# Attention with keys on partitions: a guard pass for the row maximum, row sums from TensorE, and no DMA transposes

## The chip, the core and the metric

One core of one Trainium2 chip. The metric is the device time of one execution in microseconds; the kernel before takes 1498.41 us, the median of three runs (1491.61 to 1501.3). Engines are named as the profile names them: PE (TensorE matmul; PEld its weight loads), DVE (VectorE), ACT (ScalarE), POOL (GpSimd), SP (SyncE, which here only issues DMAs).

## What is computed

One encoder layer for one sequence of 1024 tokens, width 1024, all in float32. After a conditioned RMSNorm, one projection feeds two groups of eight heads: latent attention (query and key of 96, value of 64, chunk-causal over all keys) and band attention (head size 64, nine chunks of 64 keys, with a relative-position bias). Both use

```
s = einsum('bqhd,bkhd->bhqk', q, k) * scale    (+ bias in the band)
s = where(mask, s, -1e30)
o = einsum('bhqk,bkhd->bqhd', softmax(s), v)
```

An output projection and a gated MLP with a short convolution (inner width 2816) follow. The change touches the attention alone.

## The kernel before, in words

Every float32 product is made as three passes of f32r matmuls over a high and a low half (hi x hi, hi x lo, lo x hi); gemm3 (line 147) does this for the projections.

The attention stage is written as 32 units of 512 queries: 16 of the band (4 head pairs, two halves of the queries, two heads) and 16 of latent attention (8 heads, two halves). A unit has four tiles of 128 queries. For a tile, scores (line 637) makes the scores with queries on partitions: three matmul passes per run of up to 512 keys into a two-bank PSUM tile (tag S, two of them, line 659); DVE adds the bias and finds the row minimum of the negated scores (lines 670, 674, 678), ACT takes the exponential with that minimum as its bias and the row sum as its accumulator (line 684). DVE then makes 2^15/sum (lines 686, 687), POOL makes the high f16 half (line 701), DVE the low one (line 704), and one DMA transpose on SP's queue turns both so that keys lie on partitions (line 706). Three tiles later (DEPTH), values (line 710) multiplies them with V: V's high and low f16 halves are the stationary operand side by side, and the two turned halves of P pass by, 128 queries a matmul (line 717). The four tiles share one PSUM bank (tag pv); ACT and DVE add its two halves up and scale them (lines 724, 725), and the result goes to DRAM.

q and k pages are turned by PE (qk_page, line 615; tag T, one bank) and split into halves by ACT and DVE; a band page holds both heads of a pair.

Between the tiles stand fillers, generators that issue a few matmuls of other work at a time: the projections of q, k and v for later heads (f_qk, f_v), of the latents (f_m), the up-projections (f_up, two groups), and the half of the output projection that needs the band heads only (f_oca). pace (line 806) lets R_CA or R_MLA times an attention tile's estimated cost of filler follow it; need forces a filler that the next unit depends on. The order on each engine is then set when the program is built: a scheduler takes these instructions, with the priorities given by high_priority, and lays down one fixed queue for each engine. On the chip each queue runs in order.

The attention stage ends when the last latent head is done; then come the rest of the output projection (to about 787 us) and the MLP.

## Time and profile before

| | |
|---|---|
| median of three runs | 1498.41 us (1491.61 to 1501.3) |
| span of the profiled execution, which is its own time | 1494.5 us |
| PE busy | 1286.2 us, 86% |
| DVE busy | 1022.1 us, 68% |
| POOL busy | 846.2 us, 57% |
| ACT busy | 610.9 us, 41% |
| DMA queue q1 | 185.18 MB, 44.3% of 16 engines' span |
| DMA transposes | 152, issued by SP |

The profile's page has busy time for each engine, the span in 40 slices, the chain that ended last, and groups of equal instructions with their busy time, mean duration, and the idle time ahead of them with what ended it. In a group's row the tile names stand without their buffer numbers: sc and sm are scores of the band and of latent heads, Pc and Pm the exponentials, hlc and hlm the f16 halves, PTc and PTm the turned ones, pvc and pvm the value products, oc and om the results (oc is also the name of the half output projection's PSUM tile), ipq, ipv, mp, qu, ku the fillers' products. A line such as L71, L75 or L82 is that of a helper that scales, or makes a high or a low half.

### The profile page before, as it was taken

What the parts mean: (1) busy time and instruction counts of PE and PEld (TensorE: products, weight loads), DVE (VectorE), ACT (ScalarE), POOL (GpSimd) and SP (SyncE); (2) the same over time, 40 slices, a digit from 0 to 9 for tenths busy, and PEclk for the clock granted to TensorE, in tenths of its full rate; (3) what the DMA queues carried; (4) which work ended last, traced back from release to release, by engine and by line L of the source; (5) the groups of instructions that cost most, each with busy time, mean ns of one, the idle gap of its engine ahead of it and who ended that gap; (6) DMA issues with size and microseconds to landing.
All of it is one profiled execution on the core that took longest, in us unless ns stands there. A gap on an engine that the chain in (4) does not pass through costs nothing.

```text
span 1494.5 us, 20136 instructions
## 1 busy us (share of the span) xinstructions
PE 1286.2 (86%) x6804; PEld 1067.4 (71%) x6804; DVE 1022.1 (68%) x1663; ACT 610.9 (41%) x1183; POOL 846.2 (57%) x868
## 2 busy tenths in 40 slices
PE   3789999998667888876929769999999999999997
PEld 2679878887546666664717548888888887887885
DVE  8844777756658777753576657877777787566653
ACT  5543444343445554532444224444444443333331
POOL 5664454563699744433866145655555555665662
PEclk9979989997678798977958979999999999999999
DMA  8334567554412677778521142222222234446442
GB/s 315 116 80 94 116 133 160 134 115 98 96 36 52 145 151 168 157 139 263 178 86 57 69 145 83 85 85 85 85 85 82 78 130 167 150 142 244 149 141 98
DMA packets 218738, 186.45 MB, mean 125 GB/s; under 512 B 148102, under 2 KB 183050, under 8 KB 218636
## 3 DMA queue, kind: packets, MB, share of 16 engines
q1 hardware_dynamic: 218636, 185.18, 44.3%
q8 instruction: 53, 0.87, 0.2%
q14 instruction: 49, 0.40, 0.1%
HBM read 121.69 MB, written 28.84 MB: 101 GB/s over the span
## 4 chain that ended last, share of the span: by engine, by line
PE 27%; POOL 13%; DMA 12%; DVE 12%; issue 8%; ACT 2%; SPq 1%; DVEq 0%; POOLq 0%; ACTq 0%
POOL wds L82 4%; PE p L967 3%; PE p L965 3%; PE p L966 3%; DMA wu<-w_up 3%; DMA PTm<-hlm 3%; PE dnp L1037 2%; PE dnp L1038 2%; PE dnp L1039 2%; DVE u L973 2%; PE sm L659 2%; DVE wu L995 1%; DVE u L974 1%; POOL wf L82 1%; DMA cl<-oT_d 1%
## 5 line engine op out<-in xcount | busy, mean ns | idle before, releaser
L82 POOL TENSOR_TENSOR wds<-wd,wds 128x512 fp32r<-128x512 f32 x88 | 153.3, 1760 | 99.3 <-ACT wds L75 99.3
L1037 PE MATMUL dnp<-wds,g 128*128 128x512 f32 x308 | 119.8, 391 | 3.6 <-DVE c L999 1.5
L1027 DVE TENSOR_TENSOR wd<-wd,gmbc 128x1024 f32<-128x1024 f32 x44 | 68.7, 1562 | 76.9 <-DMA wd<-w_down 76.9
L1038 PE MATMUL dnp<-wds,g 128*128 128x512 f32 x308 | 119.7, 389 | 0.0
L1039 PE MATMUL dnp<-wds,g 128*128 128x512 f32 x308 | 118.3, 389 | 0.6 <-DVE g L82 0.6
L75 ACT ACTIVATE wds<-wd 128x512 fp32r<-128x512 f32 x88 | 54.6, 624 | 150.1 <-PE dnp L1039 147.2
L82 POOL TENSOR_TENSOR wc<-ws,wc 128x512 fp32r<-128x512 f32 x22 | 56.0, 2545 | 74.2 <-ACT wc L75 74.2
L71 POOL TENSOR_SCALAR hlc<-Pc,ric 128x640 f16<-128x640 f32 (+2 forms) x64 | 48.1, 754 | 83.6 <-DVE ric L687 22.1
L71 POOL TENSOR_SCALAR hlm<-Pm,rim 128x512 f16<-128x512 f32 (+4 forms) x88 | 59.2, 676 | 62.9 <-DMA PTm<-hlm 45.8
L82 POOL TENSOR_TENSOR wa<-wu,wa 128x512 fp32r<-128x512 f32 x22 | 32.5, 1475 | 91.6 <-ACT wa L75 91.6
L659 PE MATMUL sm<-mk,mq 96*128 96x512 f32 (+3 forms) x288 | 75.8, 399 | 8.8 <-ACT Pm L684 8.4
L704 DVE SCALAR_TENSOR_TENSOR hlm<-Pm,rim,hlm 128x512 f16<-128x512 f32 (+4 forms) x88 | 66.7, 765 | 24.1 <-POOL hlm L71 23.7
L717 PE MATMUL pvm<-PTm,vt 128*128 128x128 f16 x576 | 53.2, 248 | 33.6 <-DMA PTm<-hlm 28.5
L431 DVE SCALAR_TENSOR_TENSOR aacc<-aw,cs,aacc 128x256 f32<-128x256 f32 x84 | 49.2, 586 | 47.6 <-DMA aw<-w_ada 47.1
L973 DVE SCALAR_TENSOR_TENSOR u<-c,pk,u 128x1023 f32<-128x1023 f32 x44 | 75.5, 1723 | 4.4 <-ACT u L972 4.4
L82 DVE TENSOR_TENSOR g<-gr,g 128x512 fp32r<-128x512 f32 x44 | 71.4, 1626 | 9.5 <-ACT g L75 9.5
L717 PEld LDWEIGHTS <-vt 128*128 128x128 f16 x576 | 43.0, 113 | 47.2 <-issue 45.1
L684 ACT ACTIVATE Pc<-sc,mc 128x640 f32<-128x640 f32 (+2 forms) x64 | 42.1, 659 | 76.2 <-DVE mc L674 59.1
L659 PE MATMUL sc<-k,q 64*128 64x512 f32 (+3 forms) x288 | 67.8, 364 | 2.6 <-ACT Pc L684 1.7
L1037 PEld LDWEIGHTS dnp<-wds,g 128*128 128x128 f32 x308 | 57.8, 188 | 17.2 <-ACT wds L75 1.9
L659 PEld LDWEIGHTS sm<-mk,mq 96*128 96x128 f32 x288 | 54.8, 220 | 19.4 <-ACT Pm L684 13.0
L1039 PEld LDWEIGHTS dnp<-wds,g 128*128 128x128 f32 x308 | 57.8, 188 | 13.0 <-DVE g L82 1.0
(352 smaller groups left out, 4340.9 us busy)
## 6 DMA issues: line engine op xcount, KB each, us to landing
wu<-w_up SPq DMA_DIRECT2D x44, 512.0 KB, 3.5
wd<-w_down SPq DMA_DIRECT2D x44, 512.0 KB, 3.4
aw<-w_ada SPq DMA_DIRECT2D x96, 128.0 KB, 2.3
g_d<-u SPq DMA_DIRECT2D x22, 512.0 KB, 2.6
gr<-g_d SPq DMA_DIRECT2D x44, 256.0 KB, 3.5
x<-x SPq DMA_DIRECT2D x16, 512.0 KB, 6.1
adaw<-w_ada_a SPq DMA_DIRECT2D x16, 512.0 KB, 5.0
wq_r<-w_qk SPq DMA_DIRECT2D x32, 128.0 KB, 2.6
```

Of the source, the lines that this page charges most:

```text
L71: pool.tensor_scalar(o, i, s, 1.0, op0=MUL, op1=MUL)
L75: act.activation(o, i, AF.Copy)
L82: (pool if eng == "p" else dve).tensor_tensor(o, i, f32(hi), op=SUB)
L431: dve.scalar_tensor_tensor(acc[:], w[:], cs[:, k:k + 1], acc[:], op0=MUL, op1=ADD)
L659: last = pe.matmul(s[:, c:c + w], qpg[rs_, a, q], kpgs[kh][rs_, b, ko:ko + w], start=(a == 0 and b == 0), stop=(a == 1))
L704: dve.scalar_tensor_tensor(hl[:, w:2 * w], pp, ri[:], hl[:, :w], op0=MUL, op1=SUB)
L717: last = pe.matmul(u.pv[:, c], u.vst(j), mov, start=(x == 0), stop=(x == len(todo) - 1))
L973: dve.scalar_tensor_tensor(u[:, 1:], c[:, :S - 1], pk[:, cv + 1:cv + 2], u[:, 1:], op0=MUL, op1=ADD)
L1027: dve.tensor_tensor(raw[:], raw[:], gmbc[:], op=MUL)
L1037: pe.matmul(pts[t][n], sh, w[n][:, 0], start=(j == 0), stop=False)
L1038: pe.matmul(pts[t][n], sh, w[n][:, 1], start=False, stop=False)
L1039: pe.matmul(pts[t][n], sl, w[n][:, 0], start=False, stop=(j == NF - 1))
```

## The change

Scores are made with keys on partitions, so that P needs no turning. For that the row maximum has to be known ahead:

- guard: for each tile of 128 queries one pass hi x hi over its keys, with queries on partitions as before, into one two-bank tile (tag S, now one buffer). In the band a bias in f32r is added by an identity matmul. DVE writes the tile's minimum into a column of mz.
- mrow: four PE transposes turn these columns into one row, and ACT writes it, with the logarithm of PSCALE, into a further row of the query page; the key page holds ones there, so that a score matmul subtracts the maximum.
- st: for each block of 128 keys one PSUM bank (tag ST, two buffers) of up to 512 queries. A band head stacks k's high and low half on 128 partitions against q's high half twice, so that two passes do; bias (two halves) and mask are matmuls too. A latent head takes three passes, and a mask matmul on the diagonal. ACT takes the exponential of the bank into f32; every second block it takes it a second time into f16 as high half, for the others POOL copies it. DVE makes the low half. P is not normalised.
- val: V's page holds [v, ones] in high and [v, zeros] in low, so that the value product, with up to 512 queries as moving operand and three passes, also makes the row sums. At a unit's end ACT takes Ln and then Exp of minus that for 1/sum, and DVE scales the result.
- prep: band pages are now made for each head by itself; the guard, the row and the pages of the next unit are issued among the blocks of the present one. A unit's queries use one of two page buffers, keys one of three.
- DEPTH, R_CA and R_MLA have other values; the rotary tables move to another pool; the start's PSUM tiles are shared out anew; the second band bias table is an input of its own; f_oca waits for the last band value product; an instruction asks for an activation table that holds both Exp and Ln.

The core of the diff (removed lines are shown where they are short; scores and values above are the removed functions):

```diff
-DEPTH = 3
-OFF_S, OFF_P, OFF_V = 400, 200, 200
-P_BUFS, HL_BUFS, PT_BUFS, TB = 3, 3, 3, 1
-MODE_C = "1111"
-MODE_M = "1111"
-PSCALE, VSCALE = 2.0 ** 15, 2.0 ** 14
-R_CA, R_MLA = 1.9, 0.5
+DEPTH = 2
+OFF_S, OFF_V = 400, 200
+TB = 1
+HI_ON, HL_BUFS = "pa", 3
+PSCALE, VSCALE = 2.0 ** 4, 2.0 ** 14
+R_CA, R_MLA = 1.17, 0.42
...
     startp.__exit__(None, None, None)
+    act.preload_act_table_set("natural_log_exp_and_others")
...
+    def v_tile(pl, name, tag, bufs):
+        v = pl.tile([P, 4, 2, 3, 64], F16, name=name, tag=tag, bufs=bufs)
+        pool.memset(v[:, :, 0, 1], 1.0)
+        pool.memset(v[:, :, 1, 1], 0.0)
+        return v
+
+    def v_set(v, x, src, sc):
+        hi, lo = v[:, x, 0, 0:3:2], v[:, x, 1, 0:3:2]
+        act.activation(hi, src, AF.Copy, scale=sc)
+        for c in range(2):
+            dve.scalar_tensor_tensor(lo[:, c], src[:, c], sc, hi[:, c], op0=MUL, op1=SUB)
...
+    def turned(src, rows, nm):
+        pt = ps.tile([P, 512], F32, name=f"{nm}_ps", tag="T", bufs=TB)
         for j in range(4):
             pe.transpose(pt[:rows, j * P:(j + 1) * P], src(j), ident[:])
-        pg = at.tile([P, 2, 512], F32R, name=name, tag=tag, bufs=bufs)
-        if gain is None:
-            act.activation(pg[:rows, 0], pt[:rows], AF.Copy)
-            dve.tensor_tensor(pg[:rows, 1], pt[:rows], f32(pg[:rows, 0]), op=SUB)
-        else:
-            act.activation(pg[:rows, 0], pt[:rows], AF.Copy, scale=gain)
-            dve.scalar_tensor_tensor(pg[:rows, 1], pt[:rows], gain, f32(pg[:rows, 0]), op0=MUL, op1=SUB)
-        return pg
+        return pt
...
+            order = [0, 1, 2, 3] if g == 0 else ([3, 4, 2, 5, 1, 6, 0, 7] if band else list(range(8)))
+            u.blocks = [(b, max(b, 4 * g), min(b + 4, 4 * g + 3) if band else 4 * g + 3) for b in order]
...
+        def guard(u, j):
...
+                s = ps.tile([P, 1024], F32, name=f"s{u.nm}_{i}", tag="S", bufs=1)
+                last = None
+                for x, (c, ko, w, kh) in enumerate(segs):
+                    last = pe.matmul(s[:, c:c + w], u.q[:rows, 0, q], kpages[u.nm, kh][:rows, 0, ko:ko + w],
+                                     start=True, stop=True)
+                if u.band:
+                    bg = biases[u.hd][0]
+                    w = min(n, 256)
+                    pc = [(c0 + n - w, 256 - w, w)] if (n1 == 0 or n1 >= 256) else \
+                        [(c0 + n - 256, 0, 128), (c0 + n - 128, 128, 128)]
+                    for c, bo, w in pc:
+                        last = pe.matmul(s[:, c:c + w], identr[:], bg[:, bo:bo + w], start=False, stop=True,
+                                         skip_group_check=True)
+                trail.append(last.ins)
+                if u.band:
+                    if i >= 4:
+                        dve.memset(s[64:128, c0:c0 + 64], BIG)
+                else:
+                    dve.memset(s[0:64, c0 + n - 64:c0 + n], BIG)
+                dve.tensor_reduce(mz[:, QK + j:QK + j + 1], s[:, c0:c0 + n], axis=AX.X, op=MIN)
+            return sum(w / 2.4 + 12 for _, _, w, _ in segs) + (110 if u.band else 0)
+
+        def mrow(u):
+            r = u.row
+            with tc.high_priority(offset=OFF_S):
+                pt = turned(lambda j: mz[:, QK + j - r:QK + j + 1], r + 1, f"mr{u.nm}_{u.g}")
+                act.activation(u.q[r:r + 1, u.slot], pt[r:r + 1], AF.Identity, scale=-1.0, bias=nlps[r:r + 1])
+            return 4 * 110
+
+        def st(u, x):
...
+                s = ps.tile([P, 512], F32, name=f"t{nm}", tag="ST", bufs=2)
+                todo = []
+                if u.band:
+                    todo.append((0, w, kt[:, 0, kc], u.q[:, 0, qc]))
+                    todo.append((0, w, kt[:r + 1, 1, kc], u.q[:r + 1, 1, qc]))
+                    if b >= t0:
+                        bt = biases[u.hd][1]
+                        wb = min(256, w)
+                        todo += [(0, wb, identr[:], bt[:, a, :wb]) for a in range(2)]
+                    elif b + 1 >= t0:
+                        bt = biases[u.hd][1]
+                        todo += [(0, P, identr[:], bt[:, a, P:2 * P]) for a in range(2)]
+                    if t1 == b + 4:
+                        todo.append((w - P, w, mk_k[:], mk_q[:]))
+                else:
+                    todo.append((0, w, kt[:r + 1, 0, kc], u.q[:r + 1, 0, qc]))
+                    todo.append((0, w, kt[:r, 0, kc], u.q[:r, 1, qc]))
+                    todo.append((0, w, kt[:r, 1, kc], u.q[:r, 0, qc]))
+                    if b >= t0:
+                        todo.append((0, P, mk_k[:], mk_q[:]))
+                todo.append(todo.pop(1))
+                for y, (c0, c1, l, m) in enumerate(todo):
+                    last = pe.matmul(s[:, c0:c1], l, m, start=(y == 0), stop=(y == len(todo) - 1))
+                trail.append(last.ins)
+                p = at.tile([P, 512], F32, name=f"p{nm}", tag="P", bufs=2)
+                act.activation(p[:, :w], s[:, :w], AF.Exp, scale=-1.0)
+                hl = at.tile([P, 2, 512], F16, name=f"hl{nm}", tag="HL", bufs=HL_BUFS)
+                cnt[0] += 1
+                if HI_ON[cnt[0] % len(HI_ON)] == "a":
+                    act.activation(hl[:, 0, :w], s[:, :w], AF.Exp, scale=-1.0)
+                else:
+                    hi_of("p", hl[:, 0, :w], p[:, :w])
+                dve.tensor_tensor(hl[:, 1, :w], p[:, :w], hl[:, 0, :w], op=SUB)
+                u.hl[x] = hl
+            return sum(max(107, (c1 - c0) / 2.4 + 12) for c0, c1, _, _ in todo)
+
+        def val(u, x):
...
+            w1, w2 = (v[:, y, a, u.odd:u.odd + 2].rearrange("p c b -> p (c b)") for a in range(2))
+            hl = u.hl.pop(x)
+            with tc.high_priority(offset=OFF_V):
+                if x == 0:
+                    u.pv = ps.tile([P, 512], F32, name=f"pv{u.nm}_{u.g}", tag="pv", bufs=1)
+                end = x == len(u.blocks) - 1
+                pe.matmul(u.pv[:, c], w1, hl[:, 0, :w], start=(x == 0), stop=False)
+                pe.matmul(u.pv[:, c], w1, hl[:, 1, :w], start=False, stop=False)
+                last = pe.matmul(u.pv[:, c], w2, hl[:, 0, :w], start=False, stop=end)
+                trail.append(last.ins)
+                if end:
+                    ri = at.tile([P, 512], F32, name=f"ri{u.nm}_{u.g}", tag="ri", bufs=1)
+                    r0, r1 = (slice(64, 128), slice(0, 64)) if u.odd else (slice(0, 64), slice(64, 128))
+                    act.activation(ri[r0], u.pv[r1], AF.Ln)
+                    act.activation(ri[r0], ri[r0], AF.Exp, scale=-1.0)
+                    dve.scalar_tensor_tensor(ri[r0], u.pv[r0], vscale[u.vs][1][r0], ri[r0], op0=MUL, op1=MUL)
+                    sp.dma_start(u.dst_d[:, u.g * 512:(u.g + 1) * 512], ri[r0])
+            return 3 * (w / 2.4 + 3)
...
+                pt = turned(head(0), 64, f"q{p}{o}_{g}")
+                act.activation(u.q[0:64, 0], pt[0:64], AF.Copy)
+                act.activation(u.q[64:128, 0], pt[0:64], AF.Copy)
+                dve.tensor_tensor(u.q[0:64, 1], pt[0:64], f32(u.q[0:64, 0]), op=SUB)
+                pt = turned(head(128), 64, f"k{p}{o}_{g}")
+                gk = gk_ca[0:64]
+                act.activation(u.k[0:64, 0], pt[0:64], AF.Copy, scale=gk)
+                hi_of("p", u.k[0:64, 1], f32(u.k[0:64, 0]))
+                dve.scalar_tensor_tensor(u.k[64:128, 0], pt[0:64], gk, f32(u.k[0:64, 0]), op0=MUL, op1=SUB)
+            return 8 * 110
...
+    for n, u in enumerate(units):
+        tasks = []
+        if n + 1 < U:
+            v = units[n + 1]
+            tasks += [lambda v=v: ready(v)] + [lambda j=j, v=v: v.guard(j) for j in range(4)] + [v.mrow]
+        nb = len(u.blocks)
+        ratio = R_CA if u.band else R_MLA
+        for x in range(nb):
+            cost = u.st(x)
+            late.append((u, x))
+            if len(late) > DEPTH:
+                cost += value()
+            if not late[0][0].band:
+                ca_done.append(1)
+            while len(tasks) > 6 * (nb - 1 - x) // nb:
+                cost += tasks.pop(0)()
+            pace(cost, ratio)
```

275 lines of the change are left out of this document (131 added, 144 removed).

## The prediction

> **What bounds the kernel now.** I read the page's slices first, then the busy time of each engine by stage, then the costliest groups and the waits inside the attention stages, because the change touches those alone.
>
> ```profile
> span 1494.5 us, 20136 instructions
> ...
> PE   3789999998667888876929769999999999999997
> ...
> PEclk9979989997678798977958979999999999999999
> DMA  8334567554412677778521142222222234446442
> ```
>
> ```profile
> core 0: us, PE busy (x) PEld busy (x) DVE busy (x) ACT busy (x) POOL busy (x), PEclk, DMA share, GB/s
> 70.00:120.00 50.00, 39.96 (x272) 34.55 (x271) 20.99 (x67) 24.26 (x68) 28.32 (x38) 0.83 0.36 79
> 120.00:300.00 180.00, 172.25 (x1332) 153.31 (x1331) 127.87 (x369) 75.20 (x186) 88.89 (x106) 0.96 0.58 128
> 300.00:387.00 87.00, 74.80 (x415) 63.82 (x415) 54.78 (x149) 35.01 (x115) 47.50 (x99) 0.81 0.53 115
> 387.00:490.00 103.00, 72.57 (x349) 57.22 (x350) 68.66 (x177) 51.23 (x125) 87.84 (x166) 0.78 0.22 48
> 490.00:686.00 196.00, 156.43 (x1016) 125.83 (x1014) 133.22 (x324) 90.07 (x187) 93.17 (x117) 0.84 0.75 158
> ...
> 1240.00:1494.00 254.00, 240.89 (x1056) 197.85 (x1056) 150.40 (x106) 77.36 (x128) 144.71 (x84) 0.99 0.45 156
> ```
>
> Each slice is 37.4 us. Attention runs from 70 to 686 us: band attention with the projections as filler work up to 387, the up-projections (up0, up1) at 387 to 490, latent attention with the half output projection (oc) as filler behind. The reader should see that no engine bounds all of these 616 us. PE is nearly full at 120 to 300; POOL is the fullest at 387 to 490 (87.8 of 103); at 490 to 686 none is, while the DMA engines are at 0.75 and the clock at 0.84. What waits there:
>
> ```profile
> POOL hlm L71 <- DMA PTm<-hlm: 45.8, 34, 3.8
> PE pvm L717 <- DMA PTm<-hlm: 28.5, 23, 4.0
> ...
> PE pvc L717 <- DMA PTc<-hlc: 15.0, 13, 2.7
> ```
>
> So the DMA transposes hold PE for 28.5 + 15.0 us directly. The question is whether losing them is worth more than what TensorE and ScalarE get instead.
>
> **TensorE's price per matmul.** Busy time of pipelined matmuls overlaps, so I count issue time, start to start, at full clock.
>
> ```profile
> 131.25 0.28 PE L151 MATMUL ipq<-wq_s,hT 128*128 128x256 f32 x1
> 131.37 0.28 PE L152 MATMUL ipq<-wq_s,hT 128*128 128x256 f32 x1
> ...
> 246.19 0.84 PE L717 MATMUL pvc<-PTc,v 128*128 128x128 f16 x12
> ...
> 600.49 0.60 PE L619 MATMUL mq_ps<-ident,qn 128*96 128x128 f32 x4
> ```
>
> 256 columns f32: 0.12 us. 512 columns: 240.89/1056 = 0.228 (last stage above). 384: between, 0.174. 128 columns f16: (0.84-0.22)/11 = 0.056; wider f16 moving operands have no row, and I take 0.056 for each 128 columns (0.224 at 512, beside f32's 0.228). 128 columns f32, transposes too: (0.60-0.27)/3 = 0.11.
>
> **TensorE, part by part**, with counts from the two programs' instruction lists (both 30 key blocks by query tiles a band head, 36 a latent head, 528 in all):
> - Scores before: band 72 each of 128, 256, 384 and 512 columns, 72 x 0.632 = 45.5; latent 48 each of the first three and 144 of 512, 52.2. Values: 1056 x 0.056 = 59.1. Transposes of q and k: 192 x 0.11 = 21.1. Sum 178 us.
> - Guard pass after: band 48, 72, 24, 24 (bias matmuls included), 23.6; latent 16, 16, 16, 48, 17.4. Scores with keys on partitions: band two passes in place of three, but two bias and a mask matmul on many blocks, 128, 144, 48, 48, 50.7; latent 112, 48, 48, 144, 59.2. Values: three passes in place of two, 3 x 528 x 0.056 = 88.7. Transposes: 256 for q and k (a band head now has its own pages) and 128 for the row maximum, 384 x 0.11 = 42.2. Sum 282 us.
>
> That is 104 us more for PE, all inside attention. The other work there stays:
>
> ```profile
> L151 PE MATMUL ipq<-wq_s,hT 128*128 128x256 f32 x192 | 56.9, 296 | 0.0
> ...
> L151 PE MATMUL oc<-wo,ch 128*128 128x512 f32 x64 | 28.7, 451 | 4.7 <-ACT ch L75 4.6
> ...
> L151 PE MATMUL mp<-wm_h,hT 128*128 128x416 f32 x64 | 24.8, 390 | 1.3 <-ACT wm_h L75 1.3
> ...
> L151 PE MATMUL qu<-wq,latT 128*128 128x384 f32 x32 | 15.0, 470 | 4.7 <-ACT uqr L554 4.7
> ```
>
> Each stands three times (lines 151 to 153): ipq 69 us, ipv (two thirds of that) 46, mp 36, qu 17, ku 11, oc 44, small ones 6: 229. So attention's issue time goes from 407 us, 0.66 of 616, to 511, which is 0.83 of 616. **If PE's share stays under 0.83 the kernel gets slower**; that is the number to argue about.
>
> **ScalarE.** Its part of attention is 275.8 us (24.26+75.20+35.01+51.23+90.07).
>
> ```profile
> L684 ACT ACTIVATE Pm<-sm,mm 128x128 f32<-128x128 f32 x8 | 2.9, 359 | 0.1
> ...
> L684 ACT ACTIVATE Pm<-sm,mm 128x512 f32<-128x512 f32 x8 | 5.5, 685 | 12.2 <-DVE hlm L704 11.6 <-DVE rim L686 0.6
> ...
> L684 ACT ACT_TABLE_LOAD x1 | 1.3, 1283 | 0.0
> ...
> L724 ACT ACTIVATE sbc<-pvc,vabc 64x512 f32<-64x512 f32 x16 | 10.9, 683 | 9.0 <-PE pvc L717 8.8
> ...
> L622 ACT ACTIVATE q<-q_ps 128x512 fp32r<-128x512 f32 x8 | 4.7, 584 | 0.8 <-PE q_ps L619 0.8
> ```
>
> Out go the exponentials with their accumulator reads, the sb copies and the shared q and k copies, some 146 us. In come 192 exponentials (40 each of 128, 256 and 384 columns, 72 of 512) and for every second block one more into f16 (96): 161 us at 0.36 to 0.685 by width, 140 if they cost what the copy without a bias does (0.584 at 512); I take 150. Then two 0.683 operations a unit for 1/sum, 44; q and k copies per head, 30; the row maximum, 32 x 0.58 = 19. And the preload of a common table does not do what it says: the scheduler puts it ahead of the first Silu, and the list holds 68 table loads where 3 stood, two around each of the 32 logarithms. 65 x 1.283 = 83 us. ScalarE comes to about 460 us: 0.75 of 616. (The preload's own load stands beside the loading of x; bare it costs 1.3.) Each unit ends in load, Ln, load, Exp, of which 0.683 + 1.283 + 0.683 = 2.65 us fall after the last value matmul; behind them in ScalarE's queue stand the row maximum of the next unit, without which PE can't finish that unit's first scores, and the next exponentials. With two score banks PE has some 1.2 us of its own to do then, so about 2 us a unit are open where no filler stands there.
> The Trainium skill (ScalarE: Activation LUTs, "Table sets: the hidden batching unit") says that ln and exp share one set and need one load; by that ScalarE would have 83 us less, the 2.65 would be 1.37, and the sum below some 8 us less, for the six units without fillers. The instruction list decides against it here; no run shows the common set.
>
> **VectorE, GpSimd, SP.** VectorE (405.5 us of attention, the sum of its five stages) loses 256 reciprocals and scalings and gets more and narrower lo halves; GpSimd (346) loses half the passes over P. Neither gets fuller, and neither is as full as ScalarE; if one did bound, it would be at 390 to 490, which stretch 2 below counts by GpSimd. SP loses 152 transposes, so loads behind them in its queue go out earlier; the fillers they feed were not what PE waited for. Where the waits of the transposes go, the serial guard is late next: four times matmuls, memset, reduce on one score bank:
>
> ```profile
> L678 DVE TENSOR_REDUCE mm<-sm 128x1 f32<-128x1024 f32 x8 | 9.7, 1214 | 0.1
> ...
> L678 DVE TENSOR_REDUCE mm<-sm 128x1 f32<-128x640 f32 x8 | 6.5, 814 | 0.1
> ```
>
> 4 x (0.4 of matmuls + 1.0 of reduce + 0.35 for memset and handing over, an estimate) = 7 us; with q and k turned one after the other through one bank (3.2, twice 0.44 + 0.58 + 0.6) and the row (0.9) 11 us for a second-half unit, 8 for a first-half one: 19 us a head. Each guard holds back in PE's queue what stands behind it; the list has up to 29 filler matmuls between two of them, which cover it, and none in the last three heads.
>
> **The sum, in three stretches.** What share can PE hold? In its dense stretch before, 120 to 300 us:
>
> ```profile
> L151 PE MATMUL ipq<-wq_s,hT 128*128 128x256 f32 x189 | 56.0, 296 | 0.0
> ...
> L717 PE MATMUL pvc<-PTc,v 128*128 128x128 f16 x300 | 24.3, 225 | 5.1 <-DMA PTc<-hlc 5.0
> ...
> L151 PE MATMUL ipv<-wv_s,hT 128*128 128x256 f32 x64 | 19.6, 306 | 0.6 <-ACT wv_s L75 0.6
> ...
> L659 PE MATMUL sc<-k,q 64*128 64x512 f32 x48 | 18.6, 467 | 0.4 <-ACT Pc L684 0.4
> ```
>
> Lines 151 to 153 and the four widths of scores make 567 x 0.12 + 300 x 0.056 + 192 x 0.12 + 48 x 0.632 + 10 for the rest = 148 of 180 us: 0.82. That is fillers and attention mixed, as the new kernel has them through all of the band stage, so I take it; the ends are 0.66, attention's mean, and 0.95, the last stage's (240.89 of 254).
> 1. Band stage without its last unit: attention 136, fillers 154 and 4, less 14 for that unit: 279/0.82 = 340 us, and 13 for the start, as before (70 to 120 us: PE busy 40 of 50 at a clock of 0.83, some 31 of issue time, which would fill 37 at 0.82): from 70 to 423.
> 2. The up-projections, where POOL is the fullest:
>
> ```profile
> L71 POOL TENSOR_SCALAR hlm<-Pm,rim 128x512 f16<-128x512 f32 (+4 forms) x14 | 10.2, 732 | 0.4
> ```
>
> Without these 10.2 its work is 78 of the 103; I take 90, the middle. The stretch now covers the last band unit and 1.3 latent heads. To 513.
> 3. 6.7 latent heads at 146/8 = 18.3 us of PE: 3.7 with oc, (68 + 44)/0.82 = 136; three without fillers, where guard chain and the open 2 us give some 27 a head. Before, such a head took 26.5:
>
> ```profile
> 657.14 0.73 DVE L725 SCALAR_TENSOR_TENSOR om<-pvm,vabm,sbm 64x512 f32<-64x512 f32 x1
> ...
> 683.58 0.76 DVE L725 SCALAR_TENSOR_TENSOR om<-pvm,vabm,sbm 64x512 f32<-64x512 f32 x1 [6.48 <-ACT sbm L724]
> ```
>
> 136 + 81 = 217: to 730. Before it was 686, so 44 us more; what follows is unchanged. The profiled execution spans 1494.5, 3.9 under the median of 1498.4; on the median that is 1542.
>
> **Rivals.**
> - Faster (0.20): with the transposes gone PE keeps feeding itself, clock at full. For: 43 us of direct waits and a clock of 0.84 go. Against: the start, the up-projections and the last three heads have no such share, and ScalarE is fuller. At 0.88 throughout, midway between 0.82 and 0.95, 511/0.88 = 581, 35 less: 1463. It decides from a share of 0.83 on.
> - No change (0.15): a share of 0.81 to 0.85, 1483 to 1513.
> - ScalarE becomes the bound (0.20): the Ln groups sit in the queue unforeseen by the order of the other engines, and PE stands 2 us at each of the 26 units where I hid them, or the whole 3.9: 52 to 101 more, 1594 to 1643. For: 0.75 of the time is ScalarE's. Against: fillers stand behind the guards in PE's order.
>
> ```profile
> L1009 ACT ACTIVATE u<-u x22: 1057/1062/1067, 821.6 to 1250.6; 128x1024 f32<-128x1024 f32 x22
> L1009 ACT ACT_TABLE_LOAD  x1: 1283/1283/1283, 820.3 to 820.3; - x1
> ```
>
> Here the activation follows its load at once (820.3 + 1.28). The Trainium skill (ScalarE: Activation LUTs, "What ACT_TABLE_LOAD costs") adds a drain of some 1.38 us to each switch, by an estimate 90 us more on ScalarE, which would speak for this rival; this load shows none.
>
> **Numbers.** The forecast, 1513 to 1575 about 1542, has 0.45. A measurement tells about 1% from no change, 15 us. Slower by more: 0.45 + 0.20 = 0.65; within: 0.15; faster: 0.20. The range goes from 1475 into the faster case to 1600 into the ScalarE case and leaves out about a tenth at each end.
>
> **What would show it.** 68 table loads of 1.28 us; no PTm or PTc; DMA share at 490 to 686 far under 0.75; attention ending near 730; PE issue share about 0.78; first waits of PE on ScalarE (exponentials, row maximum) in place of DMA; latent heads at the end still at 26 to 28 us. I am wrong if attention ends before 670, or if PE's share stays under 0.72.

## The result and the profile after

The changed kernel takes 1673.0 us, the median of four runs (1670.4 to 1674.77), against 1499.13 us before: a ratio of 1.1185, with a 95% interval of 1.1145 to 1.1225. The forecast of 1542 had the direction and a quarter of the size; 1673 lies outside its range. The profiled execution spans 1672.8 us. One execution of a run below, with the guard's matmuls alone, fell in a slow state (1749.6 us at a granted clock of 0.73, its neighbours 1538 to 1542) and is left out.

First the page's slices of the changed kernel, each now 41.8 us (before: 37.4).

```profile
span 1672.8 us, 20053 instructions
...
PE   4699987888877787786779294999999999999997
...
PEclk9799989989788878897679597999999999999999
DMA  8211223211100202111045124222222223544542
```

PE is at nine tenths in only three slices of the attention, and the DMA row has gone down as it should. Next the busy time of each engine by stage of the changed kernel (columns as in the prediction's table). The stages end where the fillers change: the fences behind it have the first and last start of the up-projections (qu, ku) and of the half output projection (oc), and of the scaling that ends each latent unit (rim).

```profile
core 0: us, PE busy (x) PEld busy (x) DVE busy (x) ACT busy (x) POOL busy (x), PEclk, DMA share, GB/s
70.00:120.00 50.00, 36.85 (x259) 33.99 (x260) 15.76 (x39) 24.55 (x58) 27.25 (x42) 0.80 0.17 53
120.00:300.00 180.00, 157.90 (x1138) 142.63 (x1137) 100.77 (x208) 99.61 (x204) 68.54 (x102) 0.94 0.24 71
300.00:447.00 147.00, 121.67 (x721) 103.93 (x720) 71.66 (x138) 82.63 (x189) 63.16 (x142) 0.91 0.17 48
447.00:543.00 96.00, 75.11 (x350) 57.95 (x348) 67.76 (x167) 65.58 (x139) 79.65 (x157) 0.84 0.08 24
543.00:762.00 219.00, 169.81 (x752) 119.43 (x751) 96.79 (x178) 115.79 (x197) 57.84 (x77) 0.85 0.17 53
762.00:866.00 104.00, 73.07 (x289) 46.32 (x287) 43.68 (x81) 55.46 (x92) 14.64 (x22) 0.73 0.15 46
```

```profile
L152 PE MATMUL qu<-wq,latT x32: 336/340/669, 447.2 to 539.5; 128*128 128x384 f32 x32
...
L152 PE MATMUL ku<-wk,latT x16: 392/478/796, 450.6 to 541.6; 128*128 128x512 f32 x16
...
L152 PE MATMUL oc<-wo,ch x64: 389/397/984, 554.4 to 760.5; 128*128 128x512 f32 x64
...
L796 DVE SCALAR_TENSOR_TENSOR rim<-pvm,vabm,rim x16: 743/750/757, 520.8 to 863.9; 64x512 f32<-64x512 f32 x16
```

Attention ends at 866 us in place of 686, and the rest takes what it took (806.8 us against 808.5). So all of the loss is in attention. No engine is full there; the new ScalarE stands at 444 us of 796 (the sum of its six stages). What PE waited for, 70 to 866 us (us in total, times, longest):

```profile
PE sm L702 <- DVE mz L718: 24.3, 20, 2.1
PE mrm_ps L648 <- DVE mz L718: 20.2, 9, 4.1
PE sc L702 <- DVE mz L718: 18.4, 15, 4.6
PE tm L762 <- ACT qt L725: 13.8, 15, 1.8
...
PE mrc_ps L648 <- DVE mz L718: 5.4, 6, 1.4
```

Before, the first rows were DMA transposes (28.5 and 15.0 us). Now the guard leads, and these five rows are all its own: PE stands ahead of the guard's matmuls (L702) and of the row's transposes (L648) until VectorE has made the reduce before (mz, L718), and ahead of scores until ScalarE has copied the row (qt, L725). That is 82 us of direct waiting; the forecast had looked for ScalarE at the top of this list, and it is VectorE's reduces. The end of one latent unit and the start of the next show how; these are rows of the timeline of the changed kernel, ScalarE, VectorE and PE one after the other (start, duration, engine, line; in brackets the idle time before and what ended it):

```profile
821.55 1.28 ACT L794 ACT_TABLE_LOAD   x1
822.94 0.59 ACT L794 ACTIVATE rim<-pvm 64x512 f32<-64x512 f32 x1
823.55 1.28 ACT L795 ACT_TABLE_LOAD   x1
824.84 0.63 ACT L795 ACTIVATE rim<-rim 64x512 f32<-64x512 f32 x1
827.54 0.68 ACT L725 ACTIVATE qt<-mrm_ps,nlps 1x512 fp32r<-1x512 f32 x1 [2.07 <-PE mrm_ps L648]
```

```profile
825.51 0.74 DVE L796 SCALAR_TENSOR_TENSOR rim<-pvm,vabm,rim 64x512 f32<-64x512 f32 x1 [1.20 <-ACT rim L795]
826.26 0.11 DVE L717 MEMSET sm<- 64x64 f32 x1
826.41 0.69 DVE L718 TENSOR_REDUCE mz<-sm 128x1 f32<-128x512 f32 x1
```

```profile
824.36 0.50 PE L702 MATMUL sm<-kt,qt 96*128 96x512 f32 x1 [0.73 <-DVE mz L718]
...
827.15 0.35 PE L648 MATMUL mrm_ps<-ident,mz 128*97 128x128 f32 x1 [2.18 <-DVE mz L718]
828.27 0.79 PE L762 MATMUL tm<-qt,kt 97*128 97x512 f32 x1 [0.77 <-ACT qt L725]
828.87 0.41 PE L648 MATMUL mq_ps<-ident,qn 128*96 128x128 f32 x1
```

PE has made the last guard's scores at 824.86. VectorE could reduce them at once, but its queue holds the old unit's scaling (rim) first, and that waits for ScalarE's load, Ln, load, Exp until 825.47. So its memset and reduce start 1.4 us late, then the last transpose and the copy follow, and the next unit's first score pass, which carries the row, starts at 828.27. Right behind (828.87) stands the turning of q for the unit after that, through the bank that the row has just left.

### The profile page after: what moved, and what is told of

Read it like the earlier page. It is cut to its first block, busy times and chain, and to the rows that moved or that the text cites. A ratio compares the mean times of both kernels' runs of the same rounds, so it can differ in the third digit from the quotient of the medians.

```text
span 1672.8 us, 20053 instructions
## 1 busy us (share of the span) xinstructions
PE 1408.4 (84%) x6924; PEld 1136.9 (68%) x6924; DVE 1021.1 (61%) x1384; ACT 779.2 (47%) x1384; POOL 823.7 (49%) x900
## 4 chain that ended last, share of the span: by engine, by line
PE 59%; DVE 10%; POOL 9%; DMA 9%; ACT 7%; issue 6%; DVEq 0%; SPq 0%; POOLq 0%; ACTq 0%
PE p L1068 9%; PE p L1066 9%; PE p L1067 8%; DMA aw<-w_ada 4%; POOL wds L81 4%; PE tm L762 4%; PE dnp L1138 2%; PE dnp L1140 2%; PE dnp L1139 2%; PE tc L762 2%; DVE mz L718 2%; DMA cl<-oT_d 1%; DVE adaw L321 1%; DVE aacc L445 1%; PE ipq L152 1%
## 5 line engine op out<-in xcount | busy, mean ns | idle before, releaser
L762 PE MATMUL tm<-qt,kt 96*128 96x512 f32 (+7 forms) x288 | 105.8, 475 | 20.9 <-ACT qt L725 13.8
L772 DVE TENSOR_TENSOR hlm<-pm,hlm 128x512 f16<-128x512 f32 (+2 forms) x96 | 61.3, 647 | 92.1 <-ACT hlm L769 66.8
L76 POOL TENSOR_SCALAR hlm<-pm 128x384 f16<-128x384 f32 (+2 forms) x48 | 25.3, 526 | 156.0 <-ACT pm L765 130.0
L762 PEld LDWEIGHTS tm<-qt,kt 96*128 96x128 f32 (+1 forms) x288 | 63.4, 240 | 42.3 <-ACT qt L725 18.1
L81 POOL TENSOR_TENSOR wc<-ws,wc 128x512 fp32r<-128x512 f32 x22 | 50.5, 2294 | 62.2 <-ACT wc L74 62.2
L772 DVE TENSOR_TENSOR hlc<-pc,hlc 128x512 f16<-128x512 f32 (+3 forms) x96 | 54.4, 577 | 40.3 <-ACT hlc L769 23.3
L762 PE MATMUL tc<-qt,kt 128*128 128x512 f32 (+3 forms) x192 | 70.3, 386 | 10.0 <-ACT hlc L769 4.6
L1075 DVE SCALAR_TENSOR_TENSOR u<-c,pk,u 128x1022 f32<-128x1022 f32 x44 | 68.9, 1602 | 0.0
L765 ACT ACTIVATE pm<-tm 128x512 f32<-128x512 f32 (+1 forms) x96 | 46.2, 489 | 48.3 <-PE tm L762 39.0
L1073 ACT ACTIVATE u<-c,pk 128x1024 f32<-128x1024 f32 x44 | 52.3, 1236 | 31.8 <-DVE c L1106 31.8
```

Of the source, the lines that this page charges most:

```text
L81: (pool if eng == "p" else dve).tensor_tensor(o, i, f32(hi), op=SUB)
L762: last = pe.matmul(s[:, c0:c1], l, m, start=(y == 0), stop=(y == len(todo) - 1))
L772: dve.tensor_tensor(hl[:, 1, :w], p[:, :w], hl[:, 0, :w], op=SUB)
L1075: dve.scalar_tensor_tensor(u[:, 2:], c[:, :S - 2], pk[:, cv:cv + 1], u[:, 2:], op0=MUL, op1=ADD)
```

## The experiments

All times are medians; the kernel before took between 1495.4 and 1498.3 us beside these runs, and single executions of one run lie 3 to 13 us apart, so that a difference of 4 us means nothing. One more thing moves between the runs: pace lets filler follow an estimated cost, and an edit that takes a step out takes out its estimate too (for the row 440 ns a unit, which by R_CA and R_MLA is some 11 us of filler over the 32 units, an estimate). In the runs without guard or transposes fillers therefore stand at somewhat other places.

**Loads and guard, each taken away**

```
-act.activation(ri[r0], u.pv[r1], AF.Ln)
+act.activation(ri[r0], u.pv[r1], AF.Exp, scale=0.0)
```

> The logarithm of each unit is issued as an exponential of the same shape (scale 0), so that the same two operations stand there but 64 of the 68 table loads go; the output is then not normalised. The theory (the serial guard chain, four times matmuls, memset and reduce through one score bank, holds PE) gives a small gain: the loads are 2 x 1.28 us a unit behind the guard chain, at most 10 to 30 us over 32 units, 1640 to 1665. The rival (ScalarE's end of a unit holds the next one) gives the whole 64 x 1.283 = 82 us or more, 1570 to 1595.

Measured: 1652.5, 20 us less. That is what the guard theory allowed (10 to 30 us); in the changed kernel the loads are a small part of the loss.

```
 def guard(u, j):
+    return 0
...
 def mrow(u):
-        pt = turned(...)
-        act.activation(u.q[r:r + 1, u.slot], pt[r:r + 1], ...)
+        pool.memset(f32(u.q[r:r + 1, u.slot]), -math.log(PSCALE))
```

> The guard pass and the four transposes of the row maximum are left out; the row of q that carries the maximum is filled with a constant on GpSimd, and the exponentials get a scale of 0.01 so that they stay finite; exponentials, value products and the end of each unit are as in the changed kernel. PE loses 41 + 14 us of issue time. The theory (guard chain) gives 130 to 180 us less, 1495 to 1545, with PE's issue share in attention back at about 0.75. The rival (ScalarE's end of a unit) leaves most of the loss: PE's 55 us at a share of 0.64 would be given back at most, and about 30 to 60 us less is expected, 1615 to 1645.

Measured: 1523.3, 150 us less. The guard is the main cause; its 55 us of issue time would give 86 at the share of 0.64 that PE holds in attention.

> Both at once: no guard pass, no table loads in the units. If PE then holds the share of 0.82 that was forecast, attention takes (511 - 55) / 0.82 = 556 us and 13 for the start, and the kernel 1673 - (796 - 569) = 1446. If the two causes stand one behind the other, the gains of the two runs add; if each hides the other, this run gains more than their sum.

Measured: 1463.1, a ratio to the kernel before of 0.977 (0.974 to 0.980). Both go further than the sum: 210 against 150 + 20. Without a guard the loads are worth 60 us (1523 against 1463), 1.9 us for each of 32 units. The stage from 70 to the end of attention in the run without guard, then in the run without both:

```profile
70.00:717.00 647.00, 533.19 (x3107) 431.63 (x3108) 304.92 (x586) 417.34 (x847) 328.33 (x577) 0.89 0.22 64
```

```profile
70.00:656.00 586.00, 508.34 (x3106) 415.89 (x3107) 299.36 (x586) 335.03 (x783) 328.99 (x576) 0.93 0.24 70
```

The same matmuls, 82 us less of ScalarE's time, and attention ends 61 us sooner. With 457 us of issue time (the trace's matmuls by width at the prediction's prices) PE holds 0.78 of those 586 us, not far from the 0.82 of the forecast. So scores with keys on partitions, without the row maximum that a softmax needs here, are a gain of 35 us, and row maximum and loads more than eat it.

**Which part of the guard.** All of these have the constant row, except where it is said.

The first two split the guard: one drops memsets and reduces, the other the matmuls.

```
-dve.memset(s[...], BIG)
-dve.tensor_reduce(mz[...], s[...], axis=AX.X, op=MIN)
```

```
-s = ps.tile([P, 1024], F32, name=f"s{u.nm}_{i}", tag="S", bufs=1)
-last = pe.matmul(s[...], u.q[...], kpages[...], start=True, stop=True)
+s = sfix
```

> Only the guard's matmuls are kept (41 us of issue time); memsets, reduces, the transposes and the copy of the row maximum are left out, the row is a constant filled by GpSimd (scale 0.01 in the exponentials). Nothing reads the guard's bank, so PE never waits there. Against the run with no guard (1523) this shows the price of the guard's matmuls alone: 41 us at the share of 0.72 to 0.82 that PE had there is 50 to 57, 1570 to 1580, if PE's issue time counts in full; if they fall into gaps that PE has anyway, 1525 to 1545.

> The other half: the guard's memsets and reduces stay on VectorE, over a bank that PE writes once at the start, and no guard matmul, transpose or row copy is issued (constant row, scale 0.01). This shows what the reduces cost by standing in VectorE's queue between the lo halves of P that PE waits for. If VectorE's queue is the price, 40 us or more above 1523: 1560 to 1600. If it has room, 1523 to 1540.

Measured: 1541 with the matmuls alone, 18 us above no guard: most of them fall into gaps. 1515 with the reduces alone, none at all (8 us below). What the 8 us are is open. Neither the issue time nor VectorE's time is the price.

> The guard's matmuls, memsets and reduces through the one bank stay, but the four transposes of the row maximum and its copy are left out and the row is a constant (scale 0.01). PE waits for the bank as before, and nothing waits for the row. If waits for the bank make the loss (the trace of the changed kernel shows 42 us of them), this run is at 1620 to 1650, far above matmuls and reduces added up. If the row (transposes behind the last reduce, then ScalarE's copy, then the next scores: 44 us of waits in that trace) makes it, the run is near the sum of the two halves, 1575 to 1600.

Measured: 1552.6, less than either case had. Matmuls and reduces through the one bank cost 29 us together; the waits for the bank are not the loss. So it comes with the row.

```
 pt = turned(lambda j: mz[...], r + 1, ...)
-act.activation(u.q[r:r + 1, u.slot], pt[r:r + 1], ...)
+pool.memset(f32(u.q[r:r + 1, u.slot]), -math.log(PSCALE))
```

> Guard matmuls, memsets and reduces as in the changed kernel, and the four transposes of the row maximum into the bank that q and k also use; only ScalarE's copy of the row is left out, and the row is a constant (scale 0.01). Without transposes and copy the kernel took 1553, with both 1673. If the transposes make the loss (they stand in PE's order behind the last reduce, and everything behind them waits), this run is at 1630 or more. If the copy makes it (it stands in ScalarE's order ahead of exponentials, and holds the bank), only the transposes' 14 us of issue time is added: 1565 to 1580.

Measured: 1664.5. Four transposes a unit, which nothing reads, bring back 112 of the 120 us, at 14 us of issue time. The copy is innocent, and so is its engine:

```
-act.activation(u.q[r:r + 1, u.slot], pt[r:r + 1], AF.Identity, scale=-1.0, bias=nlps[r:r + 1])
+dve.tensor_scalar(u.q[r:r + 1, u.slot], pt[r:r + 1], -1.0, -math.log(PSCALE), op0=MUL, op1=ADD)
```

> The changed kernel with its result unchanged, but the copy of the row maximum is made by VectorE in place of ScalarE. If the copy costs because it stands in ScalarE's in-order queue ahead of exponentials, most of the 120 us goes: 1560 to 1600. If it costs because bank and transposes are held up until someone copies, the engine does not matter: 1650 to 1690.

Measured: 1678.1, no gain.

```
-act.activation(u.q[r:r + 1, u.slot], pt[r:r + 1], ...)
+act.activation(u.q[96:97, 1], pt[r:r + 1], ...)
...
 c = u.prep()
+pool.memset(f32(u.q[u.row:u.row + 1, u.slot]), -math.log(PSCALE))
```

> All the guard's work stays (matmuls, memsets, reduces, the transposes of the row maximum and its copy), but the copy lands in a row that nothing reads and the row that is used gets a constant on GpSimd, with a scale of 0.01 in the exponentials so that they stay finite. So nothing waits for the maximum any more. Without any guard the kernel took 1523. If the guard costs by its latency (the next unit's scores wait for the row), this run comes within its PE issue time of that: 1523 plus 55 to 67, about 1580 to 1595. If it costs by its place in the in-order queues (PE and VectorE stand at the guard's own matmuls and reduces while other work is behind them), it stays at 1640 to 1673.

Measured: 1699.6, even more than the changed kernel. This one surprised me: no score waits for the row, and nothing is won. So the chain does not cost as a latency ahead of the scores, as I had thought; what is left is that the transposes come, in PE's order and through the one bank, each behind its reduce, the fourth behind the last.

```
-tasks += [lambda v=v: ready(v)] + [lambda j=j, v=v: v.guard(j) for j in range(4)] + [v.mrow]
+tasks += [lambda v=v: ready(v), v.mrow] + [lambda j=j, v=v: v.guard(j) for j in range(4)]
```

> All of the guard's work stays, transposes, copy and the use of the row included; only the order changes: the row of a unit is turned and copied before that unit's guards, so that it carries the maxima of the unit before (scale 0.001 in the exponentials keeps them finite). Turning the row then waits for no reduce of its own unit, while bank and queues are as busy as before. If the loss is that PE comes to the transposes in its order before VectorE has made the last reduce, the 120 us of the row shrink to the issue time of the transposes: 1565 to 1590. If the shared bank or the number of instructions makes it, it stays at 1640 to 1673.

Measured: 1583.9, as the theory had it. With every instruction of the changed kernel in place and its costs for pace the same, 89 us go when the row is turned ahead of the guards. Against the run with the transposes alone, where no score waits for the row and no copy holds the bank, it is still 81 us: what costs is the transposes' place, not the scores' wait. PE's waits in the run with the transposes alone (L648 turns q, k and the row, L702 is the guard):

```profile
PE sc L702 <- DVE kt L819: 14.3, 10, 2.3
PE sm L702 <- ACT qt L834: 13.8, 6, 3.6
PE mk_ps L648 <- DVE qt L835: 11.9, 5, 4.4
PE mrm_ps L648 <- DVE mz L718: 11.0, 6, 3.3
```

and in the run with the stale row (first row, then the guard's):

```profile
PE tm L762 <- ACT hlm L769: 12.1, 5, 3.0
...
PE sc L702 <- DVE mz L718: 8.7, 9, 2.2
```

In the first, PE waits at every link of the next unit's preparation, for its q, its k and its reduces. In the second these waits are gone from the top. The starts of PE's matmuls show why. In the run with the transposes alone, a row's last transpose, the turning of the next unit's q, and that unit's first score:

```profile
836.05 0.35 PE L648 MATMUL mrm_ps<-ident,mz 128*97 128x128 f32 x1 [0.70 <-DVE mz L718]
836.47 0.65 PE L648 MATMUL mq_ps<-ident,qn 128*96 128x128 f32 x4
...
838.93 0.63 PE L762 MATMUL tm<-qt,kt 97*128 97x512 f32 x2
```

The next q is always turned right behind the row, 0.3 to 3.4 us after its last transpose in the latent units, and so only 2.5 to 13 us (median 5) ahead of its own first score; in the run with the guard's matmuls and reduces but no transposes the median is 15. So a unit's q, k, guard and row and then the next unit's q form one chain that runs on from unit to unit. In the changed kernel this chain sets the length of a head: q follows the row by 1.3 to 2.7 us, the first score follows q by 18 to 33 us, and a latent head takes 40 to 48 us where oc stands between its tiles and 42 and 38 where nothing does. With the stale row these last two take 29 and 28.

**Mends of the chain**

```
-s = ps.tile([P, 1024], F32, name=f"s{u.nm}_{i}", tag="S", bufs=1)
+s = ps.tile([P, 512], F32, name=f"s{u.nm}_{i}_{kh}", tag="S", bufs=2)
```

> The same guard pass, but each half of its columns (up to 512) in a bank of its own, two in turn, with a reduce for each and a minimum over the two: the matmuls of the next half can run while VectorE reduces the last one. If the one bank makes the chain (matmuls wait for the reduce), second-half units save some 3 us and the kernel 40 to 100 us, 1575 to 1635. If VectorE's own order or its reduces make it, nothing is saved, and 24 more reduces a head pair cost a little: 1670 to 1700.

Measured: 1641.1, 32 us less.

```
-TB = 1
+TB = 2
...
-s = ps.tile([P, 1024], F32, name=f"s{u.nm}_{i}", tag="S", bufs=1)
+s = ps.tile([P, 512], F32, name=f"s{u.nm}_{i}_{kh}", tag="S", bufs=1)
```

> The changed kernel with its result unchanged and the banks shared out in another way: one single bank for the guard (each half of its columns in turn, with a reduce for each and a minimum over the two), and two banks in place of one for the turned q, k and row maximum. If the one bank through which q, k and the row go holds the chain together, as the untied run suggests (PE waited 23 us there for the copy of the row to free the bank), it saves 30 to 80 us: 1590 to 1640. If the guard's bank is the narrower one, it gets slower than the changed kernel: 1680 to 1700.

Measured: 1631.7, 41 us less, the best of the mends: a second bank for turning q, k and row is worth more than a second one for the guard. In its trace the q of the next latent unit is turned 6 to 21 us before the row's last transpose; with one bank it always comes after. So bank and order hang together: the order that is laid down for one bank has the row in front.

```
-dve.tensor_reduce(mz[...], s[:, c0:c0 + n], axis=AX.X, op=MIN)
+dve.tensor_reduce(mz[...], s[:, c0 + n - 128:c0 + n], axis=AX.X, op=MIN)
```

> The guard's reduce reads only the last 128 columns of each tile's scores, in place of up to 1024, so that the row it makes is no maximum (scale 0.01 in the exponentials); all matmuls and waits stay. The reduces take 128 x 0.35 us or less in place of their present time. If the reduce is the long link of the chain, about 0.6 us of each of 128 links goes, up to 75 us: 1600 to 1620. If other links (matmuls at a low clock, hand-overs, the order on PE) make the chain, under 30 us goes: 1645 to 1673.

Measured: 1634.5: 38 us, half of what the long link was thought to be worth. A shorter link shortens the chain, and no more.

```
-act.activation(ri[r0], u.pv[r1], AF.Ln); act.activation(ri[r0], ri[r0], AF.Exp, scale=-1.0)
+dve.reciprocal(ri[r0], u.pv[r1])
```

> Two mends of the changed kernel that leave the result as it is: the reciprocal of the row sums on VectorE, read straight from the score sums in place of logarithm and exponential on ScalarE (so 64 table loads and 64 operations go, 32 on VectorE come), and the guard with two single banks in turn. Apart they gave 20 (loads alone) and 32 us. If they add, 1615 to 1625; if each hides part of the other, as guard and loads did (210 for both against 150 and 20), down to 1590. If VectorE's reciprocal is slow (2 us or more for 64x512), it stands in front of the guard's reduces and takes the gain back: 1640 or more.

Measured: 1637.7, no better than the split alone. Its group of reciprocals says why (count, busy us, mean ns, idle time before):

```profile
L802 DVE RECIPROCAL rim<-pvm 64x512 f32<-64x512 f32 x16 | 53.7, 3355 | 3.6 <-PE pvm L797 3.2
```

They take 3.36 us each, in VectorE's queue ahead of the next guard's reduce, as long as load, Ln, load and Exp together less 0.4.

```
-pt = turned(lambda j: mz[...], ...); act.activation(u.q[r:r + 1, u.slot], ...)
+sp.dma_start(row_d[u.n].rearrange("j p -> p j"), f32(mz[:, QK:QK + 4]))
+sp.dma_start(f32(u.q[r:r + 1, u.slot]), row_d[u.n].rearrange("(o j) p -> o (j p)", o=1))
```

> The row maximum goes to its row by two DMAs through a scratch tensor in DRAM in place of four transposes and a copy; k carries -1 and P has no scale of its own, so that the result stays the same. The next scores do wait for the row. If the loss is the row's passage through PE's and ScalarE's in-order queues and the one bank, the kernel comes near the 1553 of the run without a row: 1555 to 1590. If it is the wait for the row itself, the DMAs (two of 2 to 3 us, by the landing times of small transfers in the traces) make it longer: 1680 to 1750.

The second adds the reciprocal of the run above.

> The same, and the reciprocal of the row sums on VectorE in place of logarithm and exponential with their 64 table loads. Without a guard the loads were worth 60 us (1523 against 1463). If the row by DMA has taken the guard's chain off, the loads are worth nearly that again: 1500 to 1535, within a few per cent of the kernel before. If the chain still holds, they are worth the 20 us that they were in the changed kernel.

Measured: 1892.6 and 1916.8, far above what either case had; the reciprocal costs 24 us here. I had priced the DMAs at 2 to 3 us; rows of SP's queue and of VectorE's waits in the first of the two:

```profile
400.97 0.39 SPq L725 DMA_DIRECT2D row_d<-mz  x1
401.40 0.49 SPq L187 DMA_DIRECT2D wm_r<-w_m  x1
410.71 0.24 SPq L726 DMA_DIRECT2D qt<-row_d  x1
```

```profile
DVE mz L719 <- DMA row_d<-mz: 100.3, 15, 9.2
```

The second DMA, which waits for the first, is issued 9.7 us after it, where the first writes 512 pieces of 4 bytes. The columns of mz are held that long, so that VectorE's next reduces wait, 100 us in all; PE's scores wait 113 us for the row itself, and SP stands 257 us at the second DMAs, with other loads behind them in its queue. This run, meant to take the row out of the queues, shows the same chain with a longer link, and it can't tell these waits apart.

```
-while len(tasks) > 6 * (nb - 1 - x) // nb:
+while len(tasks) > (3, 1, 1, 0, 4, 3, 2, 1, 1, 1, 0, 0)[x if nb == 4 else 4 + x]:
```

> The changed kernel with its result unchanged; in each unit of eight blocks the next unit's four guards are put behind blocks 0 to 3 in place of 1 to 5 and the row behind block 6 as before, in each unit of four blocks the guards behind 0 and 1 and the row at the end, so that one to three blocks of scores and values lie between the last reduce and the transposes in the order that the program gives. If PE's waiting for the reduces is the loss and this order survives the scheduler, it saves 30 to 80 us: 1590 to 1645. If the scheduler moves the transposes forward again, nothing changes: 1660 to 1685.

Measured: 1668.6, 4 us less, which is nothing. PE's first waits in this run:

```profile
PE sm L702 <- DVE mz L718: 38.3, 26, 4.0
PE mrm_ps L648 <- DVE mz L718: 23.0, 15, 4.8
```

PE still comes to the transposes too early (23.0 us, 20.2 before the mend), and at the guards themselves it now waits longer. The scheduler lays the queues down by its own reckoning, and moving the calls in the program did not part the links: in 12 of the 16 latent units nothing but the third transpose stands on PE between the last guard and the fourth (9 of 16 before the mend).

**The clock**

```
+pe.matmul(pt[:, c:c + P], identr[:], mk_q[:], start=True, stop=True)
```

> When the half output projection has been used up, dummy matmuls (128 columns, identity by a mask tile, result never read) take its place as filler at the same pace, so that PE has some 45% more matmul work in the latent heads without fillers. Nothing else is changed. If those heads are slow because PE's gaps let the clock fall (0.67 at 783 to 866), they get shorter in spite of the work: 40 us a head to 33, and the kernel 1640 to 1655. If the clock only follows, the added work costs itself or hides in the gaps: 1670 to 1700.

Measured: 1682.1, 9 us more. In the changed kernel the granted clock is 0.73 at 762 to 866 us, and value products of 512 columns follow each other 0.42 us apart, then 0.22:

```profile
814.72 0.63 PE L787 MATMUL pvm<-hlm,vt 128*128 128x512 f16 x1
815.14 0.63 PE L788 MATMUL pvm<-hlm,vt 128*128 128x512 f16 x1
...
817.88 0.39 PE L787 MATMUL pvm<-hlm,vt 128*128 128x512 f16 x1
818.11 0.38 PE L788 MATMUL pvm<-hlm,vt 128*128 128x512 f16 x1
818.32 0.38 PE L789 MATMUL pvm<-hlm,vt 128*128 128x512 f16 x1
```

The Trainium skill (TensorE: Matmul & The Clock Gate, "Part 1: The HAM clock gate") says that the array runs at half its clock until it has been busy for some 3.4 us, and gives 426.7 ns from start to start for 512 columns then; the 0.42 us of these rows agrees, and the 3.4 us no run here shows. The dummy matmuls (156 of 128 columns) did not lift the clock of the tail by much:

```profile
762.00:875.00 113.00, 90.64 (x455) 69.49 (x453) 45.75 (x84) 55.46 (x94) 14.17 (x21) 0.76 0.14 42
```

0.76 against 0.73. These small fillers in the gaps neither lift the clock by much nor save time; whether a full clock would help by itself stays open, since it was not reached.

## Why the prediction was wrong, step by step

The runs put in one row, each with all that the one above has:

| kernel | us | more |
|---|---|---|
| no guard, no table loads | 1463 | |
| with the loads around Ln | 1523 | 60 |
| with the guard's matmuls | 1541 | 18 |
| with its reduces, through the one bank | 1553 | 11 |
| with the row, turned ahead of the unit's guards | 1584 | 31 |
| with the row behind the last reduce: the changed kernel | 1673 | 89 |

The order matters: taken from the changed kernel first, the loads are worth 20; the guard's chain then seems to hide the rest.

- **PE's issue time: right.** By the trace's matmuls at the prediction's prices attention holds 512 us; 511 was forecast. The price taken without a row, 0.224 for a value product of 512 columns, shows above as 0.21 to 0.23.
- **ScalarE: right.** 444 us, 460 forecast, with the 64 loads around Ln at 1283 ns. An exponential of 512 columns without a bias takes 595 ns, nearer to the copy's 584 than to the old 685.

```profile
L765 ACT ACTIVATE pm<-tm 128x512 f32<-128x512 f32 x48 | 28.1, 595 | 31.3 <-PE tm L762 28.0 <-DVE hlm L772 3.0
```

- **The share: the step that failed.** "Each guard holds back in PE's queue what stands behind it; the list has up to 29 filler matmuls between two of them, which cover it." They don't. In the dense stretch, 120 to 300 us, they nearly do (142 us of issue time in 180, 0.79 where 0.82 was taken). But over the band stage to 447 it is 0.74 (278 of 377), in the latent heads with oc 0.59 (130 of 219) and behind them 0.45 (47 of 104). I carried a share from a stretch with dense fillers into stretches where pace gives fewer, and the guard's last links (reduce, transposes, the next q) stand next to each other there, fillers or not: a latent head with oc was to take 36.8 us (136/3.7), held up by PE's issue time, and takes the 40 to 48 us of the chain. The forecast itself named 0.72 as the point below which it is wrong; attention as a whole holds 512 of 796, 0.64, no more than before.
- **The direction: right, but not by the argument.** The forecast was slower because PE got 104 us more issue time. Without guard and loads some 50 us of that are still there (457 against 407), and the kernel is 35 us faster. What made it slower were the guard's chain and the loads, which the forecast had hidden behind fillers, so the right sign is in part luck.
- **Stage by stage.** Up-projections from 447 in place of 423 (24 us), their length 96 in place of 90 (6), and the latent heads behind them 323 in place of 217 (106): 136 us, all of the miss. Over three quarters of it are stretch 3.
- **The tail heads: mis-sized.** I gave them 27 us, "still at 26 to 28". The last one takes from 825.5 to 863.9, 38 us:

```profile
863.93 0.76 DVE L796 SCALAR_TENSOR_TENSOR rim<-pvm,vabm,rim 64x512 f32<-64x512 f32 x1 [2.96 <-ACT rim L795]
```

  The guard chain was taken at 8 us for the first unit of a head and 11 for the second. From the turning of q to the first score, with PE's other work in between, the last two units take 22 and 18 us. The chain was estimated link by link, at full clock and with each engine free when its link came; here the granted clock is 0.73, a reduce stands behind rim in VectorE's queue, and k is turned 3.8 to 9.5 us after q.
- **The Ln group: right in size, wrong in place.** "about 2 us a unit are open" is what the runs without a guard show, 1.9 us, but as the mean of all 32 units, not at six. The Trainium skill (ScalarE: Activation LUTs, "Table sets: the hidden batching unit") holds that Ln and Exp share a set. This program doesn't get that: each of the 32 Ln has a load of its own and so has the Exp behind it, 64 of the 68 loads; which sets they load the trace doesn't show. The sum without them was put 8 us lower; the runs without them show 20 with the guard and 60 without.
- **The drain.** The Trainium skill (ScalarE: Activation LUTs, "What ACT_TABLE_LOAD costs") adds some 1.38 us of drain to a switch. Here Ln starts 0.11 us after its load has ended (821.55 + 1.28, then 822.94), Exp 0.01 after its own, and the first load 0.01 after the exponential ahead of it (821.26 + 0.28, then 821.55). No drain shows.
- **The rivals.** ScalarE as the bound: no, it stands at 0.56, and of PE's waits on it the row's copy is the largest, 13.8 us. Faster: it would have been, by 2.3%, had there been no guard and no loads. VectorE and GpSimd not fuller, GpSimd the fullest at the up-projections (79.65 of 96 us), DMA share down: right.
- **Where I looked past it.** The prediction counted the guard as latency (19 us a head) and as issue time, and hid both behind fillers. It did not ask what stands in PE's queue behind the row's transposes, and what shares their bank: the whole preparation of the next unit.

What stays open: the stale row takes away the wait for the reduce, not the bank, and saves 89 us; a second bank gains 41, with a narrower guard. Both hold the preparation back, and what a second bank with the wide guard would give was not measured. A guard made one unit further ahead, with its own q and k pages, wasn't tried. No version that keeps the result beat the kernel before.

## What to carry to other kernels

When a step is turned into a chain through several in-order queues (matmul, reduce, transpose, copy), ask what stands behind each link in its queue and which buffer it holds, and let the last link run ahead by a whole stage; its own work may cost little (18, 11 and 31 us here) while its place costs 89. A filler covers such a wait only if it stands behind that very link in the fixed order, so don't carry a share from the densest stretch into the others. Price a removal and an addition in both orders: here the loads were worth 20 or 60 us, by whether the guard stood.

## What the runs showed of the hardware

- A reciprocal of 64x512 on VectorE takes 3.36 us, where a scaling of the same shape takes 0.75.
- ScalarE's copy of one row of 512 takes 0.68 us (827.54 above), more than an exponential of 128 rows (0.595); the copy has a bias operand, the exponential none.
- A DMA of 512 single 4-byte elements to DRAM held the one that waits for it back for 9.7 us.
- Four transposes that nothing reads, each behind a reduce, cost 3.5 us a unit (112 us over 32), eight times their issue time of 0.44.
